# The first and last RWKV pair's steps are given other matmuls to run between

## Chip, cores and metric

The kernel runs on one core of a Trainium2 chip. The metric is the device time of one execution, in microseconds; what is compared is the median of several executions. Before the change it is 2969.81 us (three runs, 2967.9 to 2979.55).

## What is computed

Three layers follow one another on 512 tokens of width 2048: a layer with an RWKV-7 half (16 heads of 64) and an HGRN2 half (8 heads of 128), an MLA layer and a differential attention layer. Only the first one matters here:

```python
proj = einsum('btd,dc->btc', h, w_in)
o_rwkv = rwkv7(token_shift(proj[..., :RWKV_COLS]))
o_hgrn = hgrn2(proj[..., RWKV_COLS:])
y = einsum('btc,cd->btd', concat([o_rwkv, o_hgrn], -1), w_out)
h = layer_norm(ALPHA * h + y)
```

The RWKV scan is a recurrence over tokens, `S = S * w_t + (S a_t) b_t + v_t k_t`, with `o_t = S r_t`. The kernel computes it in chunks of 64 tokens, and each chunk needs the inverse of a triangular 64x64 matrix.

## The kernel before

TensorE does nearly everything that takes time: every product is three matmuls (high and low parts of both sides, `mm3`, lines 136 to 138, tile `pj`). Weights come by SP's DMA queue in units of 128x1024 into three buffers `raw`; each unit is split in two halves, `whi` by ScalarE (line 91) and `wlo` by VectorE (line 83), with four buffers of each. A block of `w_in` is two units and 48 matmuls of 512 columns; a unit of the HGRN value projection `w_i` is 48 matmuls of 256 columns.

The first layer (`rwkv_hgrn`) goes over eight RWKV pairs p (two heads each) and eight HGRN heads. For a pair, four functions:

- `rwkv_a(p)`: four blocks of `w_in` (8+p, p, 16+p, 24+p) and the elementwise work on them, with `silu` of the last one (`z`, then `s`).
- `rwkv_m`: the triangular inverses. GpSimd writes 32x32 blocks to DRAM, reads them back rearranged (`at`), does 62 small operations on `m` and `mt`, writes the result (line 1335) and reads it back as the tile `tt` (line 1339).
- `rwkv_b`: transposes and one product, in five steps.
- `rwkv_c(p)`: everything that needs the inverses, in sixteen steps: `pm` is copied from `tt` by VectorE (line 1388) and transposed (1389), multiplied (1393, copied back by ScalarE at 1395), multiplied again (1399, copied to `tt` at 1401), then lines 1414, 1426, 1438, 1442, then seven steps of a recurrence in which ScalarE makes `S` (1458) and TensorE uses it (1450, 1453), then the norm (1467) and the result `z`.

For an HGRN head: `hgrn_i` (value projection, every second head), `hgrn_a` (blocks 41+h and 33+h), `hgrn_z` (block 49+h), `hgrn_b` (scores in seven levels, lines 1580 and 1590, then lines 1601, 1603, 1607 and the norm at 1621).

`rwkv_b`, `rwkv_c` and `hgrn_b` are generators. The class `Between` holds them and each projection calls `tick()` between its matmul groups; every n-th tick runs one step. So their small operations stand between the large matmuls in each engine's queue. `drain()` runs what is left. Which instruction stands where in a queue is then decided by a scheduler in the framework; `issue_after(behind)` keeps the copy at line 1388 behind a given VectorE instruction. The engines work their queues in the order that stands there.

For pairs 0 to 6 `rwkv_c(p)` is added by `half`, before block 24+p+1 of the next pair, with one step every third tick (CE = 3). Pair 7 has no next pair: its `rwkv_c` is added before `hgrn_z(7)`, in turns with `hgrn_b(7)`, each tick one step. Then comes the output projection: `Gated.get` loads the gated outputs `og` from DRAM through the same `raw` buffers, ScalarE makes `h`, GpSimd makes `l` from them, and `proj2` runs the first two output blocks on 14 of the 16 row blocks, with two ticks in each group; the last two row blocks are the results of pair 7 (`h_79`, `l_95`) and head 7 (`h_80`, `l_96`). After that GpSimd's queue loads the residual rows `res` for the layer norm.

Of the kernel before, what the change touches and what calls it, by code (L numbers as in the profile page):

```python
# [752 lines left out]
def layers(co, w, out):  # L753
    tc, nc = co.tc, co.nc
    with ExitStack() as ctx:
# [39 lines left out]
        def begin(i, name, tick=None, drain=None, eng=None):  # L795

            h, l = gates[i].get(w[name][0], eng)
            outs = [co.psum("pj") for _ in range(2)]
            co.proj2(outs, w[name], h, l, tick, drain)
            pair[:] = h, l, outs  # L800

        def out1(bt):
            begin(0, "w_out", lambda: [bt.tick() for _ in range(2)], bt.drain, nc.gpsimd)

        rwkv_hgrn(co, w, enter1, gates[0].put, out1)


# [313 lines left out]
def rwkv_hgrn(co, w, enter, after, out):  # L1121


    nc, tc = co.nc, co.tc
# [3 lines left out]
    with ctx:  # L1128
# [60 lines left out]
        def silu(x):  # L1189

            s = tmp("s")
            dve.tensor_scalar(s, x, -40.0, None, op0=ALU.max)
            co.sigmoid(s, s, s)
            return co.tt(x, x, s, ALU.mult)
# [4 lines left out]
        bt = Between()  # L1199

        def block(i, at={}):
            if i in first:
                return first.pop(i)

            def hook(k):
                if k in at:
                    at[k]()
                bt.tick()

            ps = co.psum("pj")  # L1210
            co.proj(ps, w["w_in"][i], xh, xl, {k: lambda k=k: hook(k) for k in range(KD)})
            return ps
# [15 lines left out]
        def rwkv_a(p, half=None):  # L1228
# [54 lines left out]
            if half:  # L1283
                half()
# [6 lines left out]
            if half:  # L1291
                half(last)
# [52 lines left out]
        def rwkv_b(avt, amb, ra, bk):  # L1345

            am, bkt = amb[:, :, :, 0:128], amb[:, :, :, 128:192]


            av = avt[:, :, 0, :]  # L1350
            for dst, srct in ((av, ra[:, :, 1:3, :]), (bkt, bk)):
                for q in range(2):
                    ps = co.psum("g")
                    cq = slice(q * 4, q * 4 + 4)
                    for i in range(4):
                        nc.tensor.transpose(ps[:, i * 128:i * 128 + 128],
                                            srct[:, q * 4 + i].rearrange("p a t -> p (a t)"), co.ident)
                    if dst is av:
                        nc.scalar.copy(av[:, cq, :], ps.rearrange("p (c t) -> p c t", c=4))
                        vc = av[64:128, cq, :].rearrange("p c (j t) -> p c j t", t=64)  # L1360
                        vm = wk.tile([128, 4, 2], F32, tag="vm", name="vm", bufs=2)
                        dve.reduce_sum(vm[64:128], vc, axis=AX.X)
                        co.stt(vc, vm[64:128].unsqueeze(3).to_broadcast([64, 4, 2, 64]), -1.0 / 64, vc,
                               ALU.mult, ALU.add)
                    else:
                        nc.scalar.copy(bkt[:, :, cq, :], ps.rearrange("p (c j t) -> p j c t", c=4, j=2))
                    yield

            ps = co.psum("g")
            for c in range(8):  # L1370
                for j in range(2):
                    mm(ps[hs[j], c * 64:c * 64 + 64], lhsT=am[64:128, j, c, 64:128], rhs=av[64:128, c, hs[j]],
                       start=True, stop=True)
            for j in range(2):
                nc.scalar.copy(avt[0:64, :, 1, hs[j]], ch(ps[hs[j], :]))
            yield
# [95 lines left out]
            co.tt(z, oc, z, ALU.mult)  # L1472
            after(p, z)

        def hgrn_i(pr):

            iv = wk.tile([128, 4, 256], F32, tag="iv", name="iv", bufs=1)
            vps = [co.psum("pj") for _ in range(2)]
            for u in range(4):
                parts = co.unit(w["w_i"][pr, u], 1024)  # L1480
                for j in range(4):
                    k = u * 4 + j
                    uh, ul = co.cut(parts, j * 256, 256)
                    for a in range(4):
                        if a % 2 == 0:
                            bt.tick()
                        ts = slice(a * 128, a * 128 + 128)
                        co.mm3(vps[a // 2][:, (a % 2) * 256:(a % 2) * 256 + 256], xh[k][:, ts], xl[k][:, ts],
                               uh, ul, k == 0 and a % 2 == 0, k == 15 and a % 2 == 1)
            for a in range(2):  # L1490
                nc.scalar.copy(iv[:, 2 * a:2 * a + 2, :].rearrange("p a c -> p (a c)"), vps[a])
            return iv
# [4 lines left out]
        def hgrn_a(h):  # L1497
            hc = slice(h, h + 1)

            f = block(41 + h)  # L1500
            ls, e = tmp("ls"), tmp("e")
            co.act(e, f, AF.Abs)
            co.act(e, e, AF.Exp, scale=-1.0)
            co.act(e, e, AF.Ln, bias=1.0)
            co.stt(ls, f, 0.0, e, ALU.min, ALU.subtract)
            k = tmp("k")
            co.tt(k, ls, f, ALU.subtract)
            co.act(k, k, AF.Exp, bias=l1[:, hc])
            co.act(e, ls, AF.Abs, bias=l1a[:, hc])
            co.act(e, e, AF.Exp, scale=-1.0)  # L1510
            co.act(e, e, AF.Ln, bias=1.0)
            dve.tensor_scalar(ls, ls, l1[:, hc], la[:, hc], op0=ALU.add, op1=ALU.max)
            co.tt(ls, ls, e, ALU.add)
            b = tmp("b")
            dve.tensor_tensor_scan(b, rs128, ls, 0.0, op0=ALU.mult, op1=ALU.add)
            q = tmp("q")
            nc.scalar.copy(q, block(33 + h))
            last = silu(q)
            return b, q, k, last

        def hgrn_z(h):
            z = wk.tile([128, T], F32, tag="zh", name="z", bufs=1)
            nc.scalar.copy(z, block(49 + h))
            silu(z)
            return z
# [103 lines left out]
        st = rwkv_a(0)  # L1629
        mid = rwkv_m(*st[:2])  # L1630
        for p in range(8):
            def half(behind=None):
                bt.drain()
                if not behind:
                    avts.append(wk.tile([128, 8, 2, 128], F32, tag="avt", name="avt", bufs=1))
                    bt.add(rwkv_b(avts[0], mid[0], *st[:2]), BE)
                else:
                    bt.add(rwkv_c(p, avts[0], behind, *mid, *st), CE)

            avts = []  # L1640
            if p < 7:
                nxt = rwkv_a(p + 1, half)
            else:
                avts.append(wk.tile([128, 8, 2, 128], F32, tag="avt", name="avt", bufs=1))
                bt.add(rwkv_b(avts[0], mid[0], *st[:2]), BE)
            if p % 2 == 0:
                iv = hgrn_i(p // 2)
            *bqk, behind = hgrn_a(p)
            bt.drain()
            if p < 7:  # L1650
                st, mid = nxt, rwkv_m(*nxt[:2])
            else:
                bt.turns = True
                bt.add(rwkv_c(p, avts[0], behind, *mid, *st), 1)
            z = []
            bt.add(hgrn_b(p, iv[:, :, (p % 2) * 128:(p % 2) * 128 + 128], *bqk, z), HE if p < 7 else 1)
            z.append(hgrn_z(p))
        out(bt)


BE, CE, HE = 3, 3, 3
# [121 lines left out]
```

## Time and profile before

| what | value |
|---|---|
| median of three runs | 2969.81 us (2967.9 to 2979.55) |
| the profiled execution | 2985.1 us |
| its span, 43252 instructions | 2983.1 us |
| busy: TensorE | 2892.7 us, 97% |
| busy: VectorE, ScalarE, GpSimd | 1782.5, 1400.3, 433.4 us |
| mean granted clock of TensorE | 0.983 of full speed |

The profiled execution is 2.0 us longer than its span and 15.3 us (0.5%) above the median of the runs. Times in the trace count from the start of the span. A row of a timeline has the start, the duration, the engine, the line, and in brackets how long the engine had been idle before it and what ended that.

### The profile page before, as it was taken

The page shows a single profiled execution, that of the slowest core. Times are in us where ns is not written, and L with a number is a line of the kernel's source. Part 1 is how long each engine was busy: PE and PEld are TensorE (multiplying, and loading weights), DVE is VectorE, ACT ScalarE, POOL GpSimd, SP SyncE. Part 2 cuts the span into 40 slices and gives each one's busy share as a digit, 9 for nine tenths or more (in the row PEclk, how much of TensorE's full clock was granted, in tenths as well). Part 3 has the DMA queues.
Part 4 walks back from the last instruction along what each step waited for, and adds up shares of the span by engine and source line. Part 5 has one row for each costly group of instructions (what it writes and reads, how often), then busy time and mean ns, then how long its engine had stood idle before and what let it go on. Part 6 is the DMA issues. An engine that isn't in the chain of part 4 may idle for free.

```text
span 2983.1 us, 43252 instructions
## 1 busy us (share of the span) xinstructions
PE 2892.7 (97%) x16462; PEld 2416.9 (81%) x16462; DVE 1782.5 (60%) x3625; ACT 1400.3 (47%) x2628; POOL 433.4 (15%) x793
## 2 busy tenths in 40 slices
PE   8799999999999899899999999999999999999999
PEld 6687787787778678677888887888888888888887
DVE  7445747646565577667887886355555555555632
ACT  5344545545454442455666565244444444444521
POOL 0403303223031520340000001100000000000000
PEclk9899999999999799899999999999999999999999
DMA  4222222222222244142222225442222222222443
GB/s 176 63 90 72 84 82 83 74 79 86 79 81 84 78 159 138 57 150 77 78 82 82 78 78 169 143 140 87 92 92 85 93 93 92 82 95 92 153 144 107
DMA packets 92045, 294.49 MB, mean 99 GB/s; under 512 B 15234, under 2 KB 15666, under 8 KB 91699
## 3 DMA queue, kind: packets, MB, share of 16 engines
q1 hardware_dynamic: 73986, 246.90, 25.3%
q0 software_dynamic: 17840, 44.74, 5.2%
q8 instruction: 131, 2.15, 0.3%
q14 instruction: 88, 0.71, 0.1%
HBM read 263.95 MB, written 27.53 MB: 98 GB/s over the span
## 4 chain that ended last, share of the span: by engine, by line
PE 56%; DVE 5%; ACT 2%; issue 1%; DMA 1%; POOL 0%; DVEq 0%; POOLq 0%; ACTq 0%
PE pj L138 17%; PE pj L136 17%; PE pj L137 17%; PE g L137 1%; PE g L138 1%; PE g L136 1%; DVE rt L83 1%; PE g L210 1%; PE g L649 1%; DVE l L83 1%; PE g L209 1%; ACT sg L80 1%; DVE p L613 0%; DVE t L86 0%; DMA raw<-og 0%
## 5 line engine op out<-in xcount | busy, mean ns | idle before, releaser
L136 PE MATMUL pj<-h,whi 128*128 128x512 f32 x2848 | 1145.4, 402 | 18.5 <-ACT h L91 16.7
L137 PE MATMUL pj<-l,whi 128*128 128x512 f32 x2848 | 1119.9, 393 | 8.9 <-DVE l L83 8.9
L138 PE MATMUL pj<-h,wlo 128*128 128x512 f32 x2848 | 1119.4, 393 | 5.3 <-DVE wlo L83 5.2
L83 DVE TENSOR_TENSOR wlo<-raw,whi 128x512 fp32r<-128x512 f32 x864 | 599.2, 698 | 748.4 <-ACT whi L91 632.6
L91 ACT CAST whi<-raw 128x512 fp32r<-128x512 f32 x864 | 533.8, 619 | 898.9 <-PE pj L137 749.0
L136 PEld LDWEIGHTS pj<-h,whi 128*128 128x128 f32 x2848 | 538.7, 189 | 138.1 <-issue 19.3
L138 PEld LDWEIGHTS pj<-h,wlo 128*128 128x128 f32 x2848 | 539.3, 189 | 123.0 <-DVE wlo L83 6.9
L137 PEld LDWEIGHTS pj<-l,whi 128*128 128x128 f32 x2848 | 540.0, 190 | 116.2 <-DVE l L83 12.0
L136 PE MATMUL pj<-whi,h 128*128 128x256 f32 x768 | 221.6, 289 | 0.0
L137 PE MATMUL pj<-wlo,h 128*128 128x256 f32 x768 | 217.1, 283 | 0.0
L138 PE MATMUL pj<-whi,l 128*128 128x256 f32 x768 | 217.1, 283 | 0.0
L136 PEld LDWEIGHTS pj<-whi,h 128*128 128x128 f32 x768 | 146.9, 191 | 4.3 <-issue 1.4
L137 PEld LDWEIGHTS pj<-wlo,h 128*128 128x128 f32 x768 | 147.1, 192 | 0.8
L138 PEld LDWEIGHTS pj<-whi,l 128*128 128x128 f32 x768 | 147.1, 191 | 0.2
L83 POOL TENSOR_TENSOR gs<-gs,rs 128x512 f32<-128x512 f32 x16 | 20.4, 1288 | 683.6 <-ACT rs L80 683.6
L80 ACT ACTIVATE p<-p,mx,rq 128x128 f32<-128x128 f32 (+3 forms) x128 | 83.1, 650 | 62.6 <-DVE mx L357 62.3
L83 POOL TENSOR_TENSOR mt<-m,at 128x60 f32<-128x60 f32 (+24 forms) x248 | 90.8, 366 | 96.7 <-DMA at<-d 77.9
L83 POOL TENSOR_TENSOR m<-m,mt 128x60 f32<-128x60 f32 (+24 forms) x248 | 96.2, 388 | 19.4
L83 DVE TENSOR_TENSOR sql<-sq,sqh 128x512 fp32r<-128x512 f32 x96 | 66.3, 690 | 33.9 <-ACT sqh L91 33.9
L91 ACT CAST sqh<-sq 128x512 fp32r<-128x512 f32 x96 | 59.2, 617 | 25.2 <-DVE sq L83 15.4
L83 DVE TENSOR_TENSOR ptl<-g,pth 128x512 fp32r<-128x512 f32 (+1 forms) x96 | 45.9, 486 | 39.0 <-ACT pth L91 39.0
L80 ACT ACTIVATE rs<-rs 128x512 f32<-128x512 f32 x80 | 50.5, 631 | 31.8 <-DVE rs L86 21.2
(446 smaller groups left out, 3866.2 us busy)
## 6 DMA issues: line engine op xcount, KB each, us to landing
raw<-w_in SPq DMA_DIRECT2D x114, 512.0 KB, 3.5
raw<-b_qk SPq DMA_DIRECT2D x64, 512.0 KB, 3.5
raw<-a_in SPq DMA_DIRECT2D x50, 512.0 KB, 3.5
raw<-w_out SPq DMA_DIRECT2D x32, 512.0 KB, 3.5
raw<-a_out SPq DMA_DIRECT2D x32, 512.0 KB, 3.9
raw<-b_v SPq DMA_DIRECT2D x32, 512.0 KB, 3.5
raw<-b_g SPq DMA_DIRECT2D x32, 512.0 KB, 3.4
raw<-b_out SPq DMA_DIRECT2D x32, 512.0 KB, 4.0
```

What stands on the lines that cost most here:

```text
L80: self.nc.scalar.activation(out, in_, func, scale=scale, **kw)
L83: return (eng or self.nc.vector).tensor_tensor(out, in0=a, in1=b, op=op)
L91: self.nc.scalar.copy(hi, src)
L136: mm(out, lhsT=ahi, rhs=bhi, start=start, stop=False)
L137: mm(out, lhsT=ahi, rhs=blo, start=False, stop=False)
L138: mm(out, lhsT=alo, rhs=bhi, start=False, stop=stop)
L209: self.nc.tensor.matmul(out, lhsT=ones, rhs=h, start=True, stop=False)
L210: self.nc.tensor.matmul(out, lhsT=ones, rhs=l, start=False, stop=True)
L649: co.nc.tensor.transpose(pt[:, a * 128:(a + 1) * 128], self.P[a][:, kt * 128:(kt + 1) * 128], co.ident)
```

## The change

`rwkv_c(0)` is no longer added before block 25, but in `hgrn_i(0)`, behind its first unit, with its copy kept behind that unit's last `wlo`. `rwkv_c(7)` is no longer added before `hgrn_z(7)`, but behind it, so that its steps run between the matmuls of the output projection; `hgrn_b(7)` takes a step every second tick there instead of every tick in turns. In the output projection a group gets as many ticks as there are generators left, two at most.

```diff
         def out1(bt):
-            begin(0, "w_out", lambda: [bt.tick() for _ in range(2)], bt.drain, nc.gpsimd)
+            begin(0, "w_out", lambda: [bt.tick() for _ in bt.works[:2]], bt.drain, nc.gpsimd)
...
-        def hgrn_i(pr):
+        def hgrn_i(pr, then=None):
...
             for u in range(4):
                 parts = co.unit(w["w_i"][pr, u], 1024)
+                if then and u == 0:
+                    then()
...
                 if not behind:
...
-                else:
+                elif p:
                     bt.add(rwkv_c(p, avts[0], behind, *mid, *st), CE)
...
             if p % 2 == 0:
-                iv = hgrn_i(p // 2)
+
+                iv = hgrn_i(p // 2, None if p else
+                            lambda: bt.add(rwkv_c(p, avts[0], co.last, *mid, *st), CE))
             *bqk, behind = hgrn_a(p)
             bt.drain()
             if p < 7:
                 st, mid = nxt, rwkv_m(*nxt[:2])
-            else:
-                bt.turns = True
-                bt.add(rwkv_c(p, avts[0], behind, *mid, *st), 1)
             z = []
-            bt.add(hgrn_b(p, iv[:, :, (p % 2) * 128:(p % 2) * 128 + 128], *bqk, z), HE if p < 7 else 1)
+            bt.add(hgrn_b(p, iv[:, :, (p % 2) * 128:(p % 2) * 128 + 128], *bqk, z), HE if p < 7 else 2)
             z.append(hgrn_z(p))
+
+        bt.turns = True
+        for x in bt.works:
+            x[1] = 1
+        bt.add(rwkv_c(p, avts[0], co.last, *mid, *st), 1)
         out(bt)
```

No arithmetic is added or removed. Pairs 1 to 6 keep their order on TensorE. GpSimd's queue keeps its order but for two pairs of `l` that change places.

VectorE's queue around the first pair's copy, where raw_109 is the first unit of `w_i` and raw_110 the second (block 25's two units stand ahead of these rows), the difference:

```order
 L86 SCALAR_TENSOR_TENSOR ra<-pj,mu,ra 128x8x63
 L86 SCALAR_TENSOR_TENSOR ra<-pj,mu,ra 128x7
+L83 TENSOR_TENSOR bon<-g,ra 128x512
+L83 TENSOR_TENSOR wlo<-raw_109,whi 128x512 x2
 L1388 COPY pm<-tt 32x512
-L83 TENSOR_TENSOR bon<-g,ra 128x512
 L1389 STREAM_TRANSPOSE pm<-pm 32x512
-L83 TENSOR_TENSOR wlo<-raw_109,whi 128x512 x2
 L83 TENSOR_TENSOR wlo<-raw_110,whi 128x512 x2
 L86 SCALAR_TENSOR_TENSOR z<-pj,mu,z 128x511
```

The copy now stands behind the first unit's `wlo`, still ahead of the second unit's and of `z` of block 25. On TensorE the first product of the pair (line 1393) stood behind 15 matmuls of block 25; now it stands behind all 48 and 30 matmuls of `w_i`.

TensorE's queue around the last pair's first product before the change; `pj` with h_72 belongs to block 56, which is `hgrn_z(7)`:

```order
L138 MATMUL pj<-h_71,wlo 128x512
L136 MATMUL pj<-h_72,whi 128x512
L137 MATMUL pj<-l_88,whi 128x512
L1393 MATMUL g<-pm,am 32x32 x16
L1561 MATMUL g<-ident,kd 128x128 x4
L1569 MATMUL g<-q,k 128x128 x4
L1399 MATMUL g<-tt,pm 32x32 x16
L1580 MATMUL g<-x 128x64 x4
```

and with the change, where `pj` with h_67 and h_68 belongs to the output projection and lines 1603 to 1609 to `hgrn_b` (1601 to 1607 before):

```order
L138 MATMUL pj<-h_67,wlo 128x512
L136 MATMUL pj<-h_68,whi 128x512
L1603 MATMUL g<-att,iv 128x128
L1609 MATMUL g<-iv,kt 128x128
L1393 MATMUL g<-pm,am 32x32 x16
L1603 MATMUL g<-att,iv 128x128
L1605 MATMUL g<-qb,hS 128x128
L1609 MATMUL g<-iv,kt 128x128
```

All of block 56, the seven levels of `hgrn_b(7)` and ten matmuls of the output projection now stand ahead of line 1393. Behind the last product of the pair (line 1467) 42 matmuls of the two output blocks are left; before it was 69.

ScalarE's queue at the same place before the change, from the exponentials of the levels (`x`) on:

```order
L80 ACTIVATE x<-x 128x512 x3
L91 CAST h_65<-raw_110 128x512
L91 CAST h_66<-raw_110 128x512
L1395 COPY pm<-g 32x512
L1563 COPY kt<-g 128x512
L91 CAST h_67<-raw_108 128x512
L91 CAST h_68<-raw_108 128x512
```

and with the change:

```order
L80 ACTIVATE x<-x 128x512 x3
L1565 COPY kt<-g 128x512
L91 CAST h_65<-raw_110 128x512
L91 CAST h_66<-raw_110 128x512
L91 CAST h_67<-raw_108 128x512
L91 CAST h_68<-raw_108 128x512
L91 CAST whi<-raw_109 128x512 x2
L80 ACTIVATE x<-x 128x512 x2
L91 CAST h_69<-raw_110 128x512
L91 CAST h_70<-raw_110 128x512
L91 CAST h_71<-raw_108 128x512
L80 ACTIVATE x<-x 128x512 x2
```

The copy of `pm` (1395) has left this place; the exponentials of the last two levels now stand behind h_69 to h_71, which are the second filling of raw_110 and raw_108 with `og`.

## Rows read from the trace of the kernel before

**Rows 1.** The page: busy time of each engine.
```profile
PE 2892.7 (97%) x16462; PEld 2416.9 (81%) x16462; DVE 1782.5 (60%) x3625; ACT 1400.3 (47%) x2628; POOL 433.4 (15%) x793
```

**Rows 2.** What the instructions on tile pm waited for: us, times.
```profile
  DMA tt<-d: 24.5, 2
```

**Rows 3.** TensorE's timeline, first pair: start us, us, engine, line, tile [idle before].
```profile
111.58 0.39 PE L136 MATMUL pj<-h,whi 128*128 128x512 f32 x1
...
131.34 1.88 PE L1393 MATMUL g<-pm,am 32*32 32x32 f32 x32 [16.17 <-DVE pm L1389]
...
137.03 1.19 PE L1399 MATMUL g<-tt,pm 32*32 32x32 f32 x32
...
148.53 0.28 PE L136 MATMUL pj<-whi,h 128*128 128x256 f32 x1
...
150.21 0.28 PE L138 MATMUL pj<-whi,l 128*128 128x256 f32 x1
```

**Rows 4.** VectorE's timeline, first pair's copy, and last pair's.
```profile
129.56 0.41 DVE L1388 COPY pm<-tt 32x512 f32<-32x512 f32 x1 [16.23 <-DMA tt<-d]
...
1003.55 2.32 DVE L1388 COPY pm<-tt 32x512 f32<-32x512 f32 x1 [8.31 <-DMA tt<-d]
```

**Rows 5.** GpSimd's timeline, first pair's inverses.
```profile
109.30 0.62 POOL L83 TENSOR_TENSOR mt<-m,at 128x60 f32<-128x60 f32 x1
...
113.41 0.29 POOL L83 TENSOR_TENSOR m<-m,mt 128x54 f32<-128x54 f32 x1
...
119.23 2.08 POOL L1335 DMA_DIRECT2D d<-m  x1 [0.30 <-POOL m L83]
127.33 1.31 POOL L1339 DMA_DIRECT2D tt<-d  x2 [6.02 <-DMA d<-m]
```

**Rows 6.** TensorE's timeline, last pair: its stall, and the end of its steps.
```profile
1007.24 1.88 PE L1393 MATMUL g<-pm,am 32*32 32x32 f32 x32 [10.26 <-DVE pm L1389]
...
1059.26 0.39 PE L136 MATMUL pj<-h,whi 128*128 128x512 f32 x1
...
1074.92 1.02 PE L186 MATMUL g<-d,onesr 128*128 128x512 f32 x2
```

**Rows 7.** Windows: us, busy of PE, PEld, DVE, ACT, POOL, clock, DMA share, GB/s.
```profile
130.00:140.00 10.00, 8.66 (x81) 7.21 (x82) 2.46 (x4) 1.77 (x3) 0.00 (x0) 0.67 0.07 13
...
1030.00:1040.00 10.00, 10.00 (x54) 7.89 (x56) 5.03 (x8) 1.76 (x3) 3.67 (x3) 0.50 0.54 164
1040.00:1050.00 10.00, 9.27 (x116) 7.19 (x113) 3.00 (x3) 6.47 (x15) 5.31 (x4) 0.94 0.36 113
```

**Rows 8.** The page: the costliest groups, mean ns behind the comma, idle before.
```profile
L83 DVE TENSOR_TENSOR wlo<-raw,whi 128x512 fp32r<-128x512 f32 x864 | 599.2, 698 | 748.4 <-ACT whi L91 632.6
L91 ACT CAST whi<-raw 128x512 fp32r<-128x512 f32 x864 | 533.8, 619 | 898.9 <-PE pj L137 749.0
...
L80 ACT ACTIVATE rs<-rs 128x512 f32<-128x512 f32 x80 | 50.5, 631 | 31.8 <-DVE rs L86 21.2
```

**Rows 9.** Timelines of GpSimd and SP, last pair: low parts and loads of og.
```profile
1003.09 2.49 POOL L83 TENSOR_TENSOR l<-raw,h 128x512 fp32r<-128x512 f32 x2
...
1005.61 21.85 SPq L111 DMA_DIRECT2D raw<-og  x3
```

**Rows 10.** Loads into raw between 975 and 1060 us, from issue to landing.
```profile
DMA to landing us min/median/max: 3.3/3.6/4.1
```

**Rows 11.** TensorE's timeline, a stall in the next layer; each matmul takes 0.39 at full clock.
```profile
1283.82 0.79 PE L138 MATMUL pj<-h,wlo 128*128 128x512 f32 x1 [4.61 <-DVE wlo L83]
```

**Rows 12.** ScalarE's timeline, one step of the last pair's recurrence.
```profile
1050.81 0.31 ACT L1458 ACTIVATE S<-g,lam 128x64 f32<-128x64 f32 x1 [0.80 <-PE g L1450]
```

**Rows 13.** Last pair's result on VectorE, then the residual loads behind it.
```profile
1065.32 0.69 DVE L83 TENSOR_TENSOR l<-z,h 128x512 fp32r<-128x512 f32 x1 [0.69 <-ACT h L91]
...
1066.59 0.57 POOL L383 DMA_DIRECT2D mlacols<-cols_a  x1 [17.92 <-issue]
...
1068.45 3.45 DMA res<-xT
```

## The prediction

> **What bounds the kernel now.** I read the page first: TensorE is busy 97% of the span [rows 1], so only time in which it stands still, or works at its lower clock, can be won. Then I asked the trace where it stands still around the steps that move. The tile `pm` tells it: of eight pairs only two had to wait for the inverse's read-back, 24.5 us of VectorE time together [rows 2]. They are the first and the last pair. VectorE reaches the copy at line 1388 and stands 16.23 and 8.31 us before it [rows 4]; all that lies behind it in its queue stands too, and TensorE waits for the product at line 1393, 16.17 us [rows 3] and 10.26 us [rows 6]. For the first pair the inverse comes late by its own chain on GpSimd: the write issues at 119.23, GpSimd waits 6.02 us for it, issues the read-back at 127.33, and the copy starts at 129.56 [rows 4, 5]. Nothing of that chain moves.
>
> Then the windows, for the clock. After the first stall the granted clock means 0.67 of full speed in 130 to 140 us, while after the second it is still 0.50 (1.2 GHz) at 1030 to 1040, although TensorE is busy 10.00 of 10.00 us, and 0.94 over the next ten [rows 7], which puts its rise at 1041. The second stall therefore costs more than its 10 us: from 1007 to 1041 everything takes twice as long.
>
> **First pair, step by step.** Block 25 begins at 111.58 [rows 3]. A large matmul follows the other at 0.227 us (69 of them between 1059.26 and 1074.92 [rows 6]), so its 48 end at 122.5. Thirty matmuls of `w_i` follow at 0.12 us (15 starts between 148.53 and 150.21 [rows 3]): 126.1. There line 1393 stands now. The copy still starts at 129.56. Between copy and product lie 1.78 us before [rows 3, 4]; one VectorE operation of about 0.6 us moves out from between, so TensorE goes on at 130.75. It waits 4.65 us instead of 16.17.
>
> The change adds a second wait. ScalarE's copy at line 1395 now stands behind the three `silu` operations of `z`, and these behind VectorE's copy, transpose, two `wlo`, `z` and `s`. From the transpose's end at 130.6: two `wlo` at 0.70, `z` and `s`, which I take as 1.2 together, four ScalarE operations at 0.63 and the copy itself, 0.6 [rows 8], which is 5.7 us, so 136.3. TensorE, through with its 18 matmuls by 134, waits about 2.3 us. Behind that wait stands line 1399, which began at 137.03 before [rows 3]. So it begins 0.7 us earlier, and 24 matmuls of block 25 (5.45 us) and 48 of `w_i` (5.75 us) are already done: 11.9 us. The remaining steps go between matmuls of the other `w_i` units and of block 41; the matmuls hide them as those of other blocks do in pairs 1 to 6, and I cost them at nothing (with that cover gone, each would cost TensorE the 1 to 2 us of its copies). I take off 0.5 us for GpSimd: **11.4 us gained.** The ends are 16.2, with no wait left, and 6, if the inverse is later (below).
>
> **Last pair.** Two things go: the wait of 10.26 us, and half of the 34 us at 1.2 GHz, 17: 27.3 us [rows 6, 7]. Four things come.
>
> (a) The exponentials of levels five and six stand on ScalarE behind h_69 to h_71. These need `og` units whose buffers come free only when GpSimd has made four low parts, and GpSimd, held by the read-back of `tt` in its own queue, begins these at 1003.09, two in 2.49 us [rows 9]. The first refill issues at 1005.61 [rows 9], the second 2.5 us later; a load takes 3.6 us [rows 10], so h_71 can start at 1011.7, the exponentials end at 1013.0, and after two short VectorE operations TensorE has its level at about 1014. Its own work ahead of that (25 matmuls of block 56 still open, 5.7 us, and six small products of about 1 us each) carries it from 997 to about 1009. A new wait of 5 to 6 us; I take 5.7. Behind it in ScalarE's and VectorE's queues stand the second half of the first `w_out` unit, the `z` of head 7 and the copy of `pm`.
>
> (b) Such a wait lowers the clock: after 4.61 us of idling a matmul takes 0.79 instead of 0.39 [rows 11]. The first pair's stretch cost the difference between 0.67 and 1 over 10 us, some of it while idle. I take 2 us, with large matmuls behind the wait.
>
> (c) The pair's own steps now run with fewer large matmuls between them: two per step of the recurrence, 0.46 us, while ScalarE waits 0.80 us for each [rows 12]. I estimate that seven steps lose 0.3 us each (0.80 less 0.46), and that the copies at 1395, 1401 and 1417 come 2.5 us late, four casts of `h` at 0.62 [rows 8] that now stand ahead of them: 4.6 us.
>
> (d) The result of the pair comes later against the matmuls: 42 are left behind line 1467 instead of 69, 6.1 us less. Before, its low part is ready at 1066.0, GpSimd's queue goes on at 1066.59, the residual is loaded from 1068.45 in 3.45 us [rows 13], and the layer norm's first product starts at 1074.92 [rows 6], with all of this only just hidden. With the cover gone TensorE waits for it; of 6.1 us, 1.6 are left as cover. 4.5 us.
>
> 27.3 - 5.7 - 2 - 4.6 - 4.5 = **10.5 us gained.** The ends: each term can be nothing, which leaves 27; if the clock stays low (below), nothing is left or a little less.
>
> **Sum.** 11.4 + 10.5 = 22 us. The profiled execution goes from 2985.1 to 2963; it was 15.3 us above the median, so the median goes from 2969.8 to **2948 us**. A measurement here tells 0.5%, 15 us, from no change, so faster means below 2955.
>
> **What the skill says against it.** At 1030 to 1040 TensorE was fully busy and at half rate [rows 7]; most of the products since 1007 are small ones, of 32 or 64 rows. The Trainium skill, "TensorE: Matmul & The Clock Gate", Part 1 (The HAM clock gate), says that the monitor goes by how busy the engine is, and that the time of sustained activity, not the number of matmuls, releases the clock. By that rule the wait in (a) costs the little of (b) and the sum stands at 22; this trace disagrees for the stretch of small products, and by the trace it can cost far more, the second rival.
>
> GpSimd's operations take 0.62 us at 109.30 and 0.29 at 113.41, when VectorE has just begun to stand still [rows 4, 5]. The Trainium skill, "GPSIMD Engine Reference", section 1 (Specifications), says that GpSimd shares its SBUF interfaces with VectorE. The trace agrees. By that rule a VectorE that no longer stands still delays the inverse, which is the third rival.
>
> **Rivals.**
>
> *No new wait in the last pair.* If the `og` units land in time, (a) and (b) fall away, 7.7 us: 30 us gained, 2940. For it: the first loads are early. Against it: GpSimd's queue is unmoved and its first low part starts at 1003.09 [rows 9]. 0.12.
>
> *The clock stays low* from the new wait through the pair's small products, as it did before for 34 us [rows 7]. About 22 us of TensorE work take twice as long; about 10 of that falls into waits of (a), (c) and (d). The last pair gains nothing or 1 us instead of 10.5: 12 us in all, 2958, no measurable change. For it: the same products caused it. Against it: 13 large matmuls come right behind the new wait. 0.14.
>
> *The moved copy still waits as long*, the change not doing what it says for the first pair: while VectorE works, the last 16 operations of the inverse take 0.62 instead of 0.29 and the tile lands 5 us later. Then 6 us instead of 11.4 are gained there: 2953. Against it: VectorE has only five operations of its own before it stands at the copy again. 0.05.
>
> *Slower than before.* The clock falls already in the levels at 1000, where few large matmuls stand, and stays low until the 42 matmuls at the end, in `hgrn_b(7)` and `rwkv_c(7)`. That is 40 us of work at half rate, 40 us more, of which 12 fall into waits: 28 us against 22, so 2976. It decides from about 45 us at 1.2 GHz, against 34 before. 0.03.
>
> **How the numbers follow.** The forecast has 0.66, with its own range of 2940 to 2955: (a) and (d) are known to some 3 us each, the first pair to 2. The range for all is 2936 to 2961, which takes in all cases but the slow one and the tails. Faster: the forecast for the most part, the first rival, half of the third and a little of the second, 0.80. No change: 0.18. Slower by over 15 us: 0.02.
>
> **What would show it.** The first pair's line 1393 with a wait of 4 to 6 us instead of 16; line 1388's wait on VectorE for `tt` gone from the last pair; between 1007 and 1041 a clock above 0.50; a new TensorE wait of about 5 us on lines 1592, with ScalarE's casts of `h` ahead of the exponentials; a wait of some us at the layer norm's first product. Pairs 1 to 6 as before. It is wrong if TensorE stands over 10 us at either place, or if the windows behind the last pair's wait stay at 0.50 for more than 10 us.

## The result, and the profile after

| | before | changed |
|---|---|---|
| median, us | 2976.28 (9 runs, 2967.9 to 2981.35) | 2959.05 (9 runs, 2957.46 to 2963.34) |
| ratio to before | | 0.9941, 95% interval 0.9925 to 0.9957 |
| profiled execution: span, us | 2983.1 | 2955.6 |
| mean granted clock of that execution | 0.983 | 0.991 |

The change makes the kernel 0.6% faster, 17.2 us by the medians. Forecast were 2948 us and a gain of 22. The two profiled executions differ by 27.5 us, more than the medians, and much of what follows is about that difference.

The page of the changed kernel, its line of busy times, answers to [rows 1]: 12 us less of TensorE's time, and a little more of GpSimd's.

```profile
PE 2880.6 (97%) x16462; PEld 2405.6 (81%) x16462; DVE 1783.1 (60%) x3625; ACT 1400.7 (47%) x2628; POOL 437.9 (15%) x793
```

What the instructions on tile `pm` waited for, in us and times: one read-back of `tt` is left of two [rows 2], and TensorE's wait for it.

```profile
its engine sat idle before it (us, times) until:
  DMA tt<-d: 11.9, 1
...
  DVE pm L1389: 5.4, 1
```

TensorE's timeline of the changed kernel at the places of [rows 3, 6] (start us, us, engine, line, tile, and in brackets the idle time before it with what ended it). In the first pair line 1393 waits 5.37 us instead of 16.17, but line 1399 starts 0.7 us later than before and takes 1.91 us instead of 1.19, the duration at the lower clock. In the last pair line 1393 waits for nothing, and a new wait of 4.07 us stands at line 1582, a level of head 7; at line 1592, where one was forecast, it is 0.30 us. The layer norm's first product (line 186) comes 28.2 us earlier, and now waits 2.40 us.

```profile
131.79 1.88 PE L1393 MATMUL g<-pm,am 32*32 32x32 f32 x32 [5.37 <-DVE pm L1389]
...
137.74 1.91 PE L1399 MATMUL g<-tt,pm 32*32 32x32 f32 x32
...
994.40 1.94 PE L1582 MATMUL g<-x 128*128 128x64 f32 x8 [4.07 <-DVE x L83]
...
1003.28 0.65 PE L1592 MATMUL g<-x 128*64 128x64 f32 x8 [0.30 <-DVE x L83]
...
1006.58 1.19 PE L1393 MATMUL g<-pm,am 32*32 32x32 f32 x32
...
1033.68 0.42 PE L1467 MATMUL g<-sql,bd 128*128 128x512 f32 x1
...
1046.73 1.22 PE L186 MATMUL g<-d,onesr 128*128 128x512 f32 x2 [2.40 <-issue]
```

VectorE's timeline of the changed kernel: the first pair's copy, 0.93 us later than in [rows 4]; late in the first layer a product of 256 columns that takes 4.88 us where its neighbours of the same shape take 0.41; and the operation ahead of the layer norm's first product, which waits for the residual rows.

```profile
130.49 0.42 DVE L1388 COPY pm<-tt 32x512 f32<-32x512 f32 x1 [11.95 <-DMA tt<-d]
...
989.03 4.88 DVE L83 TENSOR_TENSOR x<-x,k 128x256 f32<-128x256 f32 x1
993.84 0.41 DVE L83 TENSOR_TENSOR x<-x,q 128x256 f32<-128x256 f32 x1
...
1045.94 0.69 DVE L86 SCALAR_TENSOR_TENSOR d<-res,pj 128x512 f32<-128x512 f32 x1 [3.85 <-DMA res<-xT]
```

GpSimd's timeline of the changed kernel at the same moment: four low parts of `og` units back to back, where [rows 9] has two.

```profile
988.68 4.95 POOL L83 TENSOR_TENSOR l<-raw,h 128x512 fp32r<-128x512 f32 x4
```

ScalarE's timeline of the changed kernel, `h_69` to `h_71` and the exponentials of the late levels behind them:

```profile
994.89 1.14 ACT L91 CAST h<-raw 128x512 fp32r<-128x512 f32 x2 [6.16 <-DMA raw<-og]
997.28 0.62 ACT L91 CAST h<-raw 128x512 fp32r<-128x512 f32 x1 [1.25 <-DMA raw<-og]
997.81 0.63 ACT L80 ACTIVATE x<-x 128x512 f32<-128x512 f32 x1
1000.01 0.63 ACT L80 ACTIVATE x<-x 128x512 f32<-128x512 f32 x1 [1.57 <-DVE x L83]
```

Windows of the changed kernel, TensorE alone (us, busy time and matmuls, granted clock, DMA share, GB/s), to be read with [rows 7]. The first pair's stretch at 0.50 (1.2 GHz) covers all of 130 to 140 in this execution and goes on to 143; that of 1010 to 1040 is gone, and one of about 7 us before 1000 has come.

```profile
120.00:130.00 10.00, 6.41 (x43) 0.97 0.42 66
130.00:140.00 10.00, 8.21 (x84) 0.50 0.18 61
140.00:150.00 10.00, 10.00 (x86) 0.85 0.14 54
990.00:1000.00 10.00, 5.93 (x24) 0.66 0.43 126
1000.00:1010.00 10.00, 9.70 (x97) 1.00 0.59 190
1010.00:1020.00 10.00, 9.35 (x95) 1.00 0.33 107
1020.00:1030.00 10.00, 10.00 (x141) 1.00 0.32 107
1030.00:1040.00 10.00, 10.00 (x52) 1.00 0.15 52
```

By the two traces the first pair gained 8.2 us (line 1313 of the next pair starts at 191.73 instead of 199.94), and the last pair 14.9: the gain is 13.3 us before it and 28.2 at the layer norm's first product. The 5 us between come from short dips of the clock at the heads, which lie elsewhere in every execution: between 150 and 980 us four windows of ten microseconds have a clock of 0.82 to 0.84 in the profile of before, and one of 0.83 in this one. 8.2 and 14.9 are more than 17.2, so at least one of the two profiled executions is not a typical one. The experiments began there. In them a median is that of the variant's own runs, a ratio is to runs of before on the same chip at that time, with its 95% interval.

### The profile page after: what moved, and what is told of

It is laid out like the page before. It is cut to its first block, busy times and chain, and to the rows that moved or that the text cites. A ratio compares the mean times of both kernels' runs of the same rounds, so it can differ in the third digit from the quotient of the medians.

```text
span 2955.6 us, 43254 instructions
## 1 busy us (share of the span) xinstructions
PE 2880.6 (97%) x16462; PEld 2405.6 (81%) x16462; DVE 1783.1 (60%) x3625; ACT 1400.7 (47%) x2628; POOL 437.9 (15%) x793
## 4 chain that ended last, share of the span: by engine, by line
PE 84%; DVE 7%; ACT 4%; DMA 2%; issue 2%; POOL 1%; DVEq 0%; POOLq 0%; ACTq 0%
PE pj L136 25%; PE pj L137 24%; PE pj L138 24%; PE g L137 1%; PE g L138 1%; PE g L1582 1%; PE g L136 1%; DVE wlo L83 1%; DVE rt L83 1%; DMA raw<-og 1%; PE g L210 1%; ACT whi L91 1%; PE g L209 1%; PE g L649 1%; PE g L1426 1%
```

## Experiments

**Before, once more.** No edit.

> The kernel before once more, to see where its executions differ from each other. Theory V1 (before itself varies: the stretch at 1.2 GHz behind the last pair's wait, 34 us in the profiled execution, is of another length in other executions): the runs lie between 2968 and 2986, and a longer run goes with a lower mean clock (1 us at 1.2 GHz instead of 2.4 costs 0.5 us, so 17 us between runs want 0.006 of mean clock, 0.983 against 0.989); if this profile falls into a shorter run, its clock is back at full speed before 1041 us. Theory V2 (all executions have the same stretches, and the profiled one was longer for another reason, loads for instance): the mean clocks agree within 0.001 and this profile shows the same 1000 to 1041 us at 0.50.

Measured: 2973.98 us, ratio 1.0 (0.9979 to 1.002). The 12 runs fall into two groups: six at 2964.5 to 2969.2 us with a mean clock of 0.989 to 0.991, six at 2978.8 to 2985.6 with 0.983 to 0.985. The groups' medians are 2968.4 and 2983.7, 15.3 us apart. This profile came from the first group. TensorE's timeline shows the same wait in it:

```profile
1003.18 1.88 PE L1393 MATMUL g<-pm,am 32*32 32x32 f32 x32 [8.75 <-DVE pm L1389]
```

but the windows behind the wait, with the columns as above, are not those of the first profile of before. In this repeat:

```profile
1000.00:1010.00 10.00, 6.82 (x85) 0.62 0.18 62
1010.00:1020.00 10.00, 10.00 (x99) 1.00 0.28 76
1020.00:1030.00 10.00, 10.00 (x130) 1.00 0.56 190
```

and in the first profile of before:

```profile
1000.00:1010.00 10.00, 2.76 (x37) 0.51 0.27 92
1010.00:1020.00 10.00, 10.00 (x74) 0.50 0.22 54
1020.00:1030.00 10.00, 10.00 (x53) 0.50 0.19 45
1030.00:1040.00 10.00, 10.00 (x54) 0.50 0.54 164
```

V1 holds. After nearly the same wait the clock is back soon in one execution, and stays at 1.2 GHz for more than 30 us in another, 53 matmuls in ten microseconds instead of 130. [rows 6, 7] come from an execution of the second kind. The groups are less sharp in more runs: of 87 runs of before made beside the experiments (these 12 among them), 16 lie at 2970.1 us or below, 50 at 2978.7 or above and 21 between, and their median is 2979.6. The two ends are what the two profiles show; no profile shows a run from between.

**The first pair alone.** The edit to the changed kernel puts the last pair's steps, and the numbers 2 that go with them, back to where they stood:

```diff
             if p < 7:
                 st, mid = nxt, rwkv_m(*nxt[:2])
+            else:
+                bt.turns = True
+                bt.add(rwkv_c(p, avts[0], behind, *mid, *st), 1)
...
-        bt.turns = True
-        for x in bt.works:
-            x[1] = 1
-        bt.add(rwkv_c(p, avts[0], co.last, *mid, *st), 1)
```

> The first pair's part alone; the last pair stays as before. Theory A (the parts add up as in the two traces, 8 to 13 us for the first pair): 8 to 13 us under before, TensorE's wait at line 1393 about 5.4 us instead of 16.2, and the last pair's wait of about 10 us for the copy of pm and the low clock behind it unchanged. Theory B (the first pair's gain is given back by the waits that follow, so the medians moved by the last pair alone): within 5 us of before.

> The first pair's part alone once more, beside the thinner order on the same chip: two groups about 15 us apart, near 2958 (clock 0.991) and near 2974 (clock 0.985), as in its first runs.

Measured: 2971.36 us, 0.9971 (0.9952 to 0.9991), and the second time 2972.03, 0.9963 (0.9945 to 0.998). The first eleven runs again lie in two groups: five at 2956.4 to 2965.5, six at 2971.4 to 2977.6, medians 2960.3 and 2974.6. Against before's groups that is 8.1 and 9.1 us. The nine runs of the second time don't: they are spread from 2957.3 to 2978.8, three of them between 2963 and 2970, so the two groups that were expected of them did not come. Theory A holds for the gain; the first pair's gain stays, whatever the last pair does. Line 1393 waits 4.41 us at the first pair (5.4 were expected) and 9.51 at the last, and both profiles show the long stretch behind the last pair's wait, 41 us.

**The last pair alone.** The reverse edit: `else` for `elif p`, and `hgrn_i(p // 2)` without `then`.

> The last pair's part alone; the first pair stays as before. By the two profiled executions it is worth 15 us; by the medians (17 in all, less 10 for the first pair) only about 7. Theory V1 (before's low clock varies): between 5 and 10 us under the median of before, with run times closer together than those of before, since the stretch that varies is gone. Theory V2: 14 to 16 us under before. Either way the first pair's line 1393 waits 16 us.

Measured: 2969.2 us, 0.9982 (0.9967 to 0.9996); 11 of 12 runs lie between 2968.1 and 2972.3. One group, where before's first group lies: the last pair's part is worth nothing against an execution whose clock comes back soon, and 14.5 us against the others. That is V1: 5 us by the ratio, 10 by the medians, and run times closer together.

**The changed kernel, once more.** No edit.

> The changed kernel once more, beside the others on one chip, for more of its executions. Theory V1 (the two groups of run times of before come from the length of the last pair's low clock): all executions in one group, 2956 to 2964 us, mean clock 0.988 to 0.992, and none near 2975. Otherwise (the two groups have another origin that the change does not touch): some executions about 15 us above the rest with a clock near 0.985.

Measured: 2958.98 us (2956.49 to 2962.16), 0.9928 (0.9914 to 0.9941). All 15 runs of the changed kernel lie within 7 us, with clocks of 0.988 to 0.992. V1 holds here too. The profile of this run corrects the first one of the changed kernel. At the first pair line 1393 waits 4.55 us, and the clock is back at 136.5 and not at 143; at the last pair it is low from 1000.1 to 1006.9, behind a wait of 3.82 us at line 1582:

```profile
131.04 1.88 PE L1393 MATMUL g<-pm,am 32*32 32x32 f32 x32 [4.55 <-DVE pm L1389]
```

```profile
130.00:140.00 10.00, 8.96 (x99) 0.67 0.21 69
140.00:150.00 10.00, 10.00 (x103) 1.00 0.21 78
...
1000.00:1010.00 10.00, 9.71 (x56) 0.66 0.43 114
```

The runs below and above whose first pair starts at the same place agree with this one: in all seven profiles other than the first, the wait is 4.4 to 5.3 us and the first pair's stretch at 1.2 GHz 6.8 us long, where it was 13.7 in the first.

**The low parts on VectorE.**

```diff
-            begin(0, "w_out", lambda: [bt.tick() for _ in bt.works[:2]], bt.drain, nc.gpsimd)
+            begin(0, "w_out", lambda: [bt.tick() for _ in bt.works[:2]], bt.drain)
```

> The change, with the low parts of the first output projection's og units made on VectorE instead of GpSimd. Theory T1 (the new wait of 4.07 us at line 1582 is VectorE's multiplication x by k, held up by four of GpSimd's low parts that run beside it, 4.88 us instead of 0.41): no VectorE multiplication of 128x256 of the levels takes over 1 us, the wait at line 1582 is under 1 us, the clock does not fall at 992 to 1000 us, and the kernel is 4 to 8 us under the changed one, less what 14 low parts of about 0.7 us cost on VectorE where TensorE waits for it. Theory T2 (ScalarE's exponentials of the late levels stand behind the casts h of units that land late): a wait of 3 us or more stays at the levels, with ScalarE's exponentials as what ended it.

Measured: 2951.79 us (2947.98 to 2956.74), 0.9924 (0.9905 to 0.9943), 7.2 us under the changed kernel's 2959. The ratios to before, 0.9924 here and 0.9928 for the changed kernel's last runs, which were on another chip, do not tell the two apart, since before's runs vary so much; the run times do: five of these six lie below all 15 of the changed kernel. No wait of TensorE of more than 0.1 us is left between 980 and 1040 us. VectorE's timeline has the product that took 4.88 us, at its old place behind the copy of the level before it:

```profile
990.52 0.44 DVE L1583 COPY_PREDICATED att<-levm,g 128x256 f32<-128x256 int32 x1 [0.62 <-PE g L1582]
990.86 0.42 DVE L83 TENSOR_TENSOR x<-x,k 128x256 f32<-128x256 f32 x1
```

and in the windows of TensorE the clock does not fall:

```profile
985.00:995.00 10.00, 10.00 (x71) 1.00 0.26 49
995.00:1005.00 10.00, 9.86 (x93) 1.00 0.54 168
```

T1 holds for the wait at line 1582. T2 is not the cause of that wait, but is not tested by itself either: ScalarE's queue changed too, and the late exponentials stand ahead of `h_69` here (993.87 us, the next cast of `h` at 1001.10).

**The first pair's steps one weight unit later.**

```diff
-                if then and u == 0:
+                if then and u == 1:
```

> The change, with the first pair's steps begun one weight unit (48 matmuls of w_i) later. Theory A (the 5.4 us that TensorE still waits at line 1393 is the inverse's read-back, which does not move, and the low clock of 130 to 140 us comes from that wait): the product at line 1393 finds its operand ready (wait under 0.5 us, at about 132 us), no wait in its place at line 1399, the clock stays at 1.00 in 130 to 150 us, and the kernel is 7 to 10 us under the changed one. Theory B (ScalarE's and VectorE's queues ahead of the copies set the pace, or the steps now crowd at the end of the head's projections): a wait of 3 us or more at line 1399 or 1450, and less than 4 us gained.

Measured: 2951.7 us (2950.27 to 2959.59), 0.9908 (0.9892 to 0.9925), 7.3 us under the changed kernel. Line 1393 starts at 132.63 without a wait, and the windows are at full clock:

```profile
120.00:130.00 10.00, 10.00 (x72) 1.00 0.62 128
130.00:140.00 10.00, 10.00 (x131) 1.00 0.31 102
140.00:150.00 10.00, 10.00 (x104) 1.00 0.17 62
```

Theory A holds. By the first profile of the changed kernel 10.9 us were to be had (5.37 of wait and half of 11.2 of work at low clock), by its second one 7.3 (4.55 and half of 5.5); the medians show what the second one says. In the last pair the wait at line 1582 was 5.08 us here.

**Both.** The two edits together.

> The later start of the first pair and the low parts on VectorE together. If the two remaining waits are separate, the gains add: 7 to 10 us for the first and 7 us for the second (2959 to 2952 in the run of the low parts alone), so 2942 to 2946 us. If one of them only moves time that is lost again behind (weights that are not there yet, for instance), it stays above 2948.

Measured: 2946.31 us (2944.58 to 2950.55), 0.9891 (0.9875 to 0.9906). 12.7 us under the changed kernel where the two alone add to 14.5: nearly separate, 0.3 us outside the bound set for that. This version is faster than both kernels.

**The first pair alone, with the low parts on VectorE.** Is it GpSimd that made the last pair's wait of before? The copy of `pm` takes 2.32 us there, beside two low parts of 2.49 in all [rows 4, 9].

> The first pair's part of the change with the low parts on VectorE; the last pair's steps where they stood before. Theory W (the last pair's wait for the inverse stands by itself, 8 us, and the clock's fall behind it lasts 8 us in some executions and 41 in others): the wait at line 1393 stays at 6 us or more, the runs fall into two groups about 15 us apart (clock near 0.991 and near 0.985) and the median is 7 us or more above the run that has both parts and the low parts on VectorE (2952). Theory G (the wait and its length came from GpSimd's queue and its low parts): the copy of pm takes 0.4 us instead of 2.4, the wait shrinks to under 5 us, and the kernel comes within 3 us of 2952, in one group.

Measured: 2970.26 us, 0.9961 (0.9941 to 0.998): three runs at 2956.0 to 2959.0 and seven at 2967.0 to 2975.5, clocks of 0.990 or more and of 0.987 or less. The copies of `pm` all take 0.42 us or less, so GpSimd had stretched the copy; but 6.86 us of wait stay, for the read-back, and with them the spread and the long stretch. Theory W.

**Thinner steps behind the wait.** In the kernel with the first pair's part alone, at first one step after six large matmuls instead of three:

```diff
-                bt.add(rwkv_c(p, avts[0], behind, *mid, *st), 1)
+                bt.add(rwkv_c(p, avts[0], behind, *mid, *st), 2)
...
-            bt.add(hgrn_b(p, iv[:, :, (p % 2) * 128:(p % 2) * 128 + 128], *bqk, z), HE if p < 7 else 1)
+            bt.add(hgrn_b(p, iv[:, :, (p % 2) * 128:(p % 2) * 128 + 128], *bqk, z), HE if p < 7 else 2)
```

> The first pair's part alone, as in the run of it, but the last pair's and head 7's steps one by one after six large matmuls instead of three from line 1393 on, so that the same wait (8 to 10 us for the copy of pm) is followed by denser work. Theory D (what follows the wait decides whether the clock comes back: in the long stretches small products stood between three large matmuls each): one group of run times near 2958 with a clock of 0.990 or more, and in the profile the clock is back within 10 us of the wait's end. Theory C (whether it comes back soon is left to chance by the wait itself, whatever follows): two groups about 15 us apart, near 2958 and near 2974, as with the first pair's part alone.

Measured: 2972.37 us, 0.9974 (0.9959 to 0.9989), 7 of 11 runs between 2969.4 and 2972.5. Neither theory's numbers. The clock was back by about 1001 us, 5 us after the wait of 8.66 us had ended, but a second wait of 3.62 us with a low clock of its own had come, again a level at line 1582. VectorE's timeline has its cause,

```profile
1014.92 5.57 DVE L83 TENSOR_TENSOR x<-b 128x256 f32<-128x256 f32 x4
```

four short subtractions that end with GpSimd's four low parts:

```profile
1014.65 5.57 POOL L83 TENSOR_TENSOR l<-raw,h 128x512 fp32r<-128x512 f32 x4 [2.14 <-ACT h L91]
```

So the run did not decide between D and C. The next one has the same two edits with the low parts on VectorE.

> The thinner order behind the last pair's wait once more (six large matmuls between two steps at first), now with the low parts on VectorE, which takes away the second wait that the first try of it met. Its partner is the first pair's part with the low parts on VectorE, whose runs fell into groups of 2956 to 2959 (clock 0.991) and 2967 to 2975 (0.985). Theory D (what follows the wait decides how long the clock stays low): a wait of 6 to 8 us stays at line 1393, the clock is back within 10 us of its end, and all runs lie in one group near 2957 to 2962, none with a clock of 0.986 or less. Theory C (the length is left to chance, whatever follows): half of the runs or more near 2972 with a clock of 0.985.

Measured: 2958.2 us, 0.9938 (0.9921 to 0.9956), six runs at 2955.7 to 2962.6, none with a clock under 0.989. Of its partner's ten runs, on another chip, seven lay in the long group. TensorE still waits at line 1393, 6.61 us until 993.10; its windows:

```profile
990.00:1000.00 10.00, 6.91 (x68) 0.53 0.12 39
1000.00:1010.00 10.00, 10.00 (x89) 1.00 0.58 159
1010.00:1020.00 10.00, 9.83 (x74) 1.00 0.79 245
```

Those of its partner (6.86 us until 991.87, and three large matmuls between the steps):

```profile
990.00:1000.00 10.00, 8.13 (x84) 0.50 0.07 27
1000.00:1010.00 10.00, 10.00 (x56) 0.50 0.01 2
1010.00:1020.00 10.00, 10.00 (x51) 0.50 0.13 25
1020.00:1030.00 10.00, 10.00 (x115) 0.76 0.51 181
```

Theory D, as far as six runs tell: with the wait nearly as long, what TensorE does behind it decides how likely a long stretch is. In both profiles of the thinner order the stretch at 1.2 GHz is 10.2 us long; in the three of the tighter order with the same first pair it is 37.6 to 41. That it is the spacing and not another detail of the order, and why the tighter order gives a long stretch in some executions and a short one in others, is left open.

## Why the prediction was right, and where not

The time, 2959.05, lies in the range for all cases (2936 to 2961) and the direction was the forecast one, but it lies outside the forecast's own range of 2940 to 2955. The point of 2948 was 11 us too low, nearly all of it from one step.

*The sum was taken from the wrong execution.* This is the step that failed: "the profiled execution goes from 2985.1 to 2963; it was 15.3 us above the median, so the median goes from 2969.8 to 2948". The 17 us for "half of the 34 us at 1.2 GHz" exist only in executions with the long stretch. Two of the three runs of before that were shown were of the other kind, and so was their median (2969.8, beside 2968.4 and 2983.7 for the groups). The 15.3 us between the profiled execution and that median were about what that stretch costs: by the two profiles of before 33.9 and 4.5 us of work ran at half rate behind the wait, and half the difference is 14.7. Its gain was subtracted from a median that did not contain it. By groups: about 8.5 us from either for the first pair; for the last pair nothing from the short ones and 14.5 from the long ones. 2968.4 less 8.5 is 2959.9, and the changed kernel's median is 2959.05. Three runs were also too few: the median of the 87 later runs of before, 2979.6, less the 22 us of the sum gives 2957.6, only 1.4 us from what was measured.

*First pair, 11.4 forecast; 8.2 in the first trace of the changed kernel, 10 to 12 in seven others, 8 to 9 in the medians.* The wait was forecast at 4.65: it was 5.37 in that trace, where the inverse ended 0.9 us later, and 4.4 to 5.3 in the seven other profiles with this start. The second wait, forecast at 2.3, is in none of them: TensorE's 18 matmuls, which the sum took at full clock, ran at half rate and filled the time up to line 1399. That line was to begin 0.7 us earlier than before; it began 0.7 later in the first trace and between 0.8 earlier and 0.7 later in the others. What the sum left out is the clock. Before, TensorE stood still through most of its low stretch, and from 131.3 only 5.3 us of work ran at half rate, until the clock rose at 136.6. In the first trace of the changed kernel the clock falls at 129.4, when the shorter wait is more than half over, and rises at 143.0, so 11.2 us of work run at half rate, 3 us more time than before. But this is that execution alone: in the seven others 4.9 to 6.7 us of work run at half rate, about as much as before, and line 1313 of the next pair starts 10 to 12 us earlier than in the first profile of before. There the sum held. Why the medians show only 8 to 9 of it is open. The run with the later start took the wait and the low stretch away.

*Last pair, in the executions with the long stretch: 10.5 forecast, about 15.* (a) A new wait of 5.7 us was forecast, and 4.07 measured, but at line 1582 and not at 1592, and for another reason, so that the size came near by luck. TensorE waited for VectorE, which GpSimd's low parts held. ScalarE did stand 6.16 us before `h_69` as described, and its late exponentials came at 997.81 and 1000.01; line 1592 waited only 0.30 us behind them, since TensorE itself was held up by the wait at line 1582 and the clock behind it. What the late exponentials would have cost without that wait, no run shows. The row that could have told of GpSimd's hold on VectorE stood in [rows 4]: a copy of `pm` of 2.32 us instead of 0.41, beside two low parts [rows 9]. I had read GpSimd's slowness under VectorE from [rows 4, 5], and not the reverse. The Trainium skill, "SBUF — State Buffer", section "SBUF: two separate sides", says that a VectorE operation with two inputs in SBUF, as this one, and a GpSimd operation take a shared pair of ports as an exclusive lock, so that one of them stands for the whole instruction of the other. The trace agrees in that the product ends just behind GpSimd's work, at 993.91 and 993.63. It goes further: 4.88 us is the time of four low parts of 1.24 us each, not of one. (b) 2 us for the clock were 2.7, half of the 5.4 us of work from 994.4 to 999.8, and 3.3 in the second profile. (c) 4.6 us for thinly covered steps were under 1: the pair's own products wait for nothing, and head 7's norm at line 1623 waits 0.48 and 0.17 us. (d) 4.5 us for the late result were 2.40, with VectorE waiting for the residual rows as forecast, and behind it a clock of 0.63 from 1048 to 1052.

*Rivals.* The inverse slowed by a busier VectorE came as 0.9 us in the first trace of the changed kernel, not 5; in the seven others the copy starts between 0.3 us earlier and 1.0 later than before. That the clock stays low behind the new wait did not happen in either profile of the changed kernel: it was low for 6.8 us, 993.0 to 999.8 and 1000.1 to 1006.9. That rival's 2958 us agree with the result by chance only. The run with the low parts on VectorE stands for the first rival, without the new wait: by the medians it gained 7.2 us where 7.7 had been set for it.

## What to carry over

Before a term is taken from a stretch of low clock, look whether every execution has it: run times that go with two mean clocks say that it does not, and a gain read from the longer kind must not be subtracted from a median of the shorter. The same holds for the changed kernel: one profile of it put 3 us on the first pair that seven other profiles with the same start do not have. After a wait that stays, it helped here to place more large matmuls between the small products. A helper engine's batch must be set against what VectorE does on the critical path at that time, not against the helper's own idle time.

## What was not expected of the hardware

After a wait of 8.75 us at line 1393 the clock stayed at 1.2 GHz for 10 us in one execution of before, and after one of 10.26 us for 41 us in another, with the same instructions; the length of the wait does not sort them, since another kernel's 6.86 us had 37.6 us behind them. The two groups of twelve run times lie 15.3 us apart. With six large matmuls between the first steps instead of three, and the low parts on VectorE, none of six executions had a mean clock as low as the long stretch gives. And a VectorE operation of 0.41 us took 4.88, 5.90 and 4.66 us in three kernels beside a run of GpSimd's low parts. It ended only with the run's last operation, although each of these is 1.24 us long.
